# Half of the odd layer's weight sums made during the attention, six loads issued earlier, three adds moved to DVE

## The chip, the cores and the metric

The program runs on one core of a Trainium2 chip. The metric is the device time of one execution in microseconds. PE is the matrix engine; its weight loads (PEld) overlap with its matmuls. DVE, ACT and POOL are the vector, scalar and general engines. SP issues nearly all transfers. Each engine takes its instructions strictly in the order that was fixed when the program was built; semaphores alone hold it back.

## What is computed

Two layers on x of 1024 tokens by 1024 features, all in float32.

- Even layer: one input projection gives a_x, a_g, q, k, v, g. Path A puts a_x through a causal convolution of width 4 and a gated linear recurrence (RG-LRU, 8 blocks of 128 features). Path B is stick-breaking attention in 8 heads of 128. Each path is multiplied by its SiLU gate, and both together go through an output projection of 2048 by 1024.
- Odd layer: grouped-query attention in a window of 128 tokens (16 heads of 64, 2 key and value heads), gated, and an output projection of 1024 by 1024.
- After each layer x becomes LayerNorm(alpha * x + sublayer(x)), with a gain and a bias that are read from memory.

```
h = _rg_lru(_causal_dwconv(a_x, conv_w, conv_b), ...) * silu(a_g)
o = _stick_breaking(q, k, v) * silu(g)
x = _layer_norm(alpha * x + concat(h, o) @ w_out, g0, b0)
x = _layer_norm(alpha * x + _odd_layer(x) @ w_out_odd, g1, b1)
```

## The kernel before, in words

**Numbers.** Every product is made of three matmuls: each operand is split into a high part h (a cast on ACT) and a remainder l (a subtraction on DVE or POOL), and `mm3` adds h·h, h·l and l·h in one PSUM bank. A typical matmul is 128x128 by 128x512.

**Stages.** (1) Loading x and the first v products. (2) The recurrence: `lru_main(f)` for f = 0 to 7 makes gates and scan of block f, while PE is filled from a queue (`fill`) with the projections of block f+1 (`lru_proj`) and products for v (`v_tiles`). A projection fills a PSUM bank `pj_ax` or `pj_ag`; ACT reads it into `xc` (L489), DVE adds three shifted copies (L494), and the bank is free again. There are three such banks. (3) `attn_all`: 8 heads, whose 12 units each run scores `z`, sigmoid tiles B and C, a scan on C, B times C (L381, DVE), transposes `tr` (L389, PE), and products `pv` with v; the fill queue holds the projections k, q and g of the next head, and in head 7 the beginning of the output projection (`early_out`). (4) The output projections, in seven products of block sums (as in Strassen's scheme), into banks `opeX`, `opeZ` (even) and `opoX`, `opoZ`, `opoY` (odd), each followed by a LayerNorm. Between them lies the odd attention.

**Sums of weights.** The seven products need sums of blocks of the output weights. `odd_parts()` makes those of the odd layer in four groups t = 0 to 3: it loads four blocks into `oqta` and `oqtb`, makes sums and differences on POOL (L286 to L299), splits seven of them (`part`: cast on ACT L263, subtraction on POOL L264), and stores each in memory (`stoB..`, `stoT..`), from where the odd output projection reads them. The split parts lie in tiles with the tag `wt`, two at a time. The generator is advanced at each of the 32 steps of the recurrence, so all four groups stand in stage (2).

**First operands.** `prep(k)` loads the pair `opwh`, `opwl` of a step of the even output projection (512 KB each for k below 8, L575). `early_out()` is a generator in the fill queue of head 7; its first act is prep(0) to prep(7).

**Last norm.** `norm(s)` for the row tile s (128 tokens) takes the statistics (L711, L724 on DVE), the factors `rs` (L727, L728), scales on ACT (L732), multiplies by the gain on POOL (L733, 128x1024), and adds the bias one tile later in `shift()` (L718, 128x1024, on POOL in the last norm). The order is 4, 5, 6, 7, 0, 1, 2, 3; tile 3 alone is finished in pieces (L733 and L737 on POOL, L740 and L744 on DVE). The gain and bias lie in `gb2`.

The order of each engine's instructions is decided by a scheduler from the program and its own estimate of times, so a line that is moved in the code moves more than itself.

Of the kernel before, what the change touches and what calls it, by code (L numbers as in the profile page):

```python
# [13 lines left out]
F32R = mybir.dt.float32r  # L14
# [4 lines left out]
P = 128  # L19
S = 1024  # L20
D = 1024
# [31 lines left out]
def trunk(ctx, tc, x, xT_in, w_even, w_even_v, w_even_out, w_gate, lru_vec,  # L53
          e_ln, w_odd, sinks, w_odd_out, o_ln, out):
    nc = tc.nc
# [10 lines left out]
    def slot(name, dtype):  # L66
        return slots.tile([P, 2, HALF], dtype, tag="s", name=name)
# [200 lines left out]
    def odd_parts():  # L268

        sub = partial(nc.gpsimd.tensor_tensor, op=ALU.subtract)  # L270
        for t in range(4):
            p1, p2 = slot(f"oq{t}a", F32), slot(f"oq{t}b", F32)
            b11, b12, b21, b22 = p1[:, 0, :], p1[:, 1, :], p2[:, 0, :], p2[:, 1, :]
            for tile_, dm, e in ((b22, 1, 4 + t), (b12, 1, t), (b11, 0, t), (b21, 0, 4 + t)):
                nc.sync.dma_start(tile_, w_odd_out[dm, e])
            hold = []

            def part(kind, raw):
                if not hold:
                    two = yt("wt", [P, 2, 2, HALF], f"op{kind}{t}")  # L280
                    hold.extend([two[:, 0], two[:, 1]])
                stash_parts(kind, t, raw, hold.pop(), nc.gpsimd)

            part("oB22", b22)
            yield
            sub(out=b22, in0=b22, in1=b12)  # L286
            part("oT3", b22)
            yield
            part("oB11", b11)
            yield  # L290
            sub(out=b12, in0=b12, in1=b11)
            part("oT1", b12)
            yield
            nc.gpsimd.tensor_tensor(out=b11, in0=b22, in1=b11, op=ALU.add)
            part("oT2", b11)
            yield
            part("oB21", b21)
            yield
            sub(out=b21, in0=b21, in1=b11)  # L299
            part("oT4", b21)  # L300
            yield
            yield
# [43 lines left out]
    def attn_all():  # L346
# [8 lines left out]
        def u_stage(n, i, g):  # L355
            W = min(HALF, (i + 1) * P - g * HALF)
            z = bank("z", f"z{n}_{i}_{g}")
            qh, ql = qk["q", n, i // 4]
            kh, kl = qk["k", n, g]
            c = (i % 4) * P  # L360
            diag = (i // 4 == g)
            a, b = qh[:, c:c + P], ql[:, c:c + P]
            nc.tensor.matmul(z[:, :W], a, kh[:, :W], start=True, stop=False)
            nc.tensor.matmul(z[:, :W], a, kl[:, :W], start=False, stop=False)
            nc.tensor.matmul(z[:, :W], b, kh[:, :W], start=False, stop=True)
            if diag:
                nc.vector.tensor_tensor(out=z[:, W - P:W], in0=z[:, W - P:W], in1=mask, op=ALU.add)  # L367
            B = wt_("B", f"B{n}_{i}_{g}", F32)
            C = wt_("C", f"C{n}_{i}_{g}", F32, HALF + 1)
            nc.scalar.activation(C[:, :W], z[:, :W], AF.Sigmoid, scale=-SC)  # L370
            nc.scalar.activation(B[:, :W], z[:, :W], AF.Sigmoid, scale=SC)
            if diag:
                nc.gpsimd.memset(C[:, W:W + 1], 1.0)
                init = 1.0
            else:
                nc.vector.tensor_copy(C[:, W:W + 1], carry[n, i])
                init = carry[n, i]
            cr = C[:, 0:W][:, ::-1]
            nc.vector.tensor_tensor_scan(cr, cr, one.broadcast_to([P, W]), init, ALU.mult, ALU.mult)  # L379
            carry[n, i] = C[:, 0:1]  # L380
            nc.vector.tensor_tensor(out=B[:, :W], in0=B[:, :W], in1=C[:, 1:W + 1], op=ALU.mult)  # L381
            wsb[n, i, g] = B
# [41 lines left out]
        for idx in range(len(units) + LAG + 1):  # L424
            while vpend:
                v_stage(*vpend.pop(0))
            if idx < len(units):
                n, i, g = units[idx]
                if (i, g) == (NS - 2, 1) and n < 7:
                    w_sums(n + 1, w_even_out, 8)  # L430
                if n == 0 and (i, g) == (2, 0):
                    w_sums(0, w_even_out, 8)
                if (i, g) == (NS - 1, 1):
                    fill.drain()
                    load_ya(n)
                    fill.add(gate_proj(n, 1))
                    if n + 1 < SB_HEADS:
                        load_v(n + 1)
                        fill.add(gate_proj(n, 0), head_proj(n + 1))
                        rate[0] = 31.2 / 12  # L440
                        if n + 2 == SB_HEADS:
                            fill.add(gate_proj(n + 1, 0))
                            rate[0] = 36.4 / 12
                    else:
                        fill.add(early_out())
                        rate[0] = 20.8 / 12
                u_stage(n, i, g)
                pend.append(units[idx])
            if idx >= LAG and pend:
                n, i, g = pend.pop(0)  # L450
                t_stage(n, i, g)
                if i % 2 == 0 and g == 0:
                    vpend.append((n, i // 2))
            yield
# [182 lines left out]


    def early_out():
        for t in range(8):  # L640
            prep(t)
        for p in range(3):
            op[0, p] = bank(XB[p], f"opeX{p}")
        for t in range(8):
            for p in range(3):
                step_mm(t, p)
                yield C_512
# [18 lines left out]
    for f in range(8):  # L666
        q, sts = VT[f]
        if f == 2:
            for d in range(ND):
                load_wv(1, d)  # L670
        if f + 1 < 8:
            if f == 2:
                fill.add(lru_proj(f + 1), v_tiles(q, sts))
            else:
                fill.add(v_tiles(q, sts[:1]), lru_proj(f + 1), v_tiles(q, sts[1:]))
        else:
            fill.add(v_tiles(q, sts))
            load_v(0)
            fill.add(head_proj(0))
        r = (5.2 * len(sts) + 20.8) / 4  # L680
        for _ in lru_main(f):
            fill.pump(r)
            next(odd_w, None)
        fill.drain()
    for _ in attn_all():
        fill.pump(rate[0])
# [12 lines left out]
    def out_norms(lnp, gb, after, name, final):  # L699
# [13 lines left out]
        def shift():  # L713
            if pend:
                s = pend.pop()
                xt = xpre[:, s, :]
                eng = nc.gpsimd if final else nc.vector
                eng.tensor_tensor(out=xt, in0=xt, in1=gb[:, 1, :], op=ALU.add)  # L718
                after(s, slice(0, D))

# [352 lines left out]

    ep = ctx.enter_context(tc.tile_pool(name="epool", bufs=1, reuse_waits="tile"))
    gb2 = ep.tile([P, 2, D], F32, name="gb2")
    nc.sync.dma_start(gb2, o_ln.rearrange("(o a) d -> o a d", o=1).broadcast_to([P, 2, D]))
    put, norm, shift = out_norms(
        ep, gb2, lambda s, cs: nc.sync.dma_start(out[s * P:(s + 1) * P, cs], xpre[:, s, cs]), "o", True)

# [8 lines left out]
    y_diffs_odd()  # L1088
    for k in range(8, 12):
        prep_odd(k)  # L1090
    for p in range(4):
        evac_odd(0, p)
    for p in range(4):
# [72 lines left out]
```

## Time and profile before

| what | value |
|---|---|
| median of 3 runs | 1264.69 us (1263.58 to 1265.02) |
| profiled execution | 1261.55 us, of which the traced span is 1259.7 us |
| mean granted TensorE clock | 0.992 of full speed |
| PE busy | 1217.9 us, 97% of the span |
| DVE, POOL, ACT busy | 864.8 us (69%), 707.8 us (56%), 646.5 us (51%) |
| stage 2, the recurrence | about 60 to 333 us from the span's start |
| from the end of PE's last matmul to the end of the span | 1246.5 to 1259.7 us, 13.2 us |
| POOL in the last norm | at work without a break from 1220.1 to 1250.7 us |
| stage 3, one head of attention | 50.25 us (head 1: 401.86 to 452.11 us) |

The span is the time from the first to the last traced instruction; the 1.85 us beside it are start and end of the program. A share of 97% is a mean: where PE has no work that is ready, the stretch shows it, and that is what the rows further down are about.

### The profile page before, as it was taken

Reading aid. Unit: us, or ns where it says so; the run is one execution under the profiler, and the core shown is the slowest. Engines: PE = TensorE matmul, PEld = TensorE weight load, DVE = VectorE, ACT = ScalarE, POOL = GpSimd, SP = SyncE. Lnnn points to the kernel's source line nnn. Section 1 sums busy time; section 2 is a strip of 40 time slices with the busy share of each in tenths; the row PEclk is TensorE's granted clock in tenths of the full one; section 3 lists DMA queues with packets and bytes.
Section 4 is the critical chain, followed back from the end, with each engine's and each line's share of the span. In section 5 each row is a group of like instructions: output and inputs, shape, how many; then the busy total and the mean of one; then the engine's idle time right before and its main releaser. Section 6 shows DMA issues by size and latency. Waiting matters only on the chain.

```text
span 1259.7 us, 18357 instructions
## 1 busy us (share of the span) xinstructions
PE 1217.9 (97%) x6104; PEld 1027.3 (82%) x6104; DVE 864.8 (69%) x1589; ACT 646.5 (51%) x1309; POOL 707.8 (56%) x758
## 2 busy tenths in 40 slices
PE   8999989899999999999999999999999999999895
PEld 6788768688888888888888788888888888888684
DVE  7655656656677767677676848877447766666886
ACT  6355566666534434344343437443457776667432
POOL 3554578754474665564543258767256665544428
PEclk9999999999999999999999999999999999999998
DMA  8422655542654352552544789811010111104633
GB/s 293 196 77 89 237 213 209 197 138 89 204 167 134 134 178 74 176 179 76 183 138 153 280 319 334 263 49 50 26 51 27 34 35 34 43 1 135 233 120 132
DMA packets 95998, 179.50 MB, mean 142 GB/s; under 512 B 10912, under 2 KB 28704, under 8 KB 95648
## 3 DMA queue, kind: packets, MB, share of 16 engines
q1 hardware_dynamic: 95904, 178.34, 41.4%
q8 instruction: 48, 0.79, 0.3%
q14 instruction: 46, 0.38, 0.1%
HBM read 119.58 MB, written 58.72 MB: 142 GB/s over the span
## 4 chain that ended last, share of the span: by engine, by line
PE 85%; DVE 6%; DMA 3%; ACT 2%; issue 1%; POOL 1%; SPq 0%; POOLq 0%; ACTq 0%; DVEq 0%
PE tr L389 2%; PE pj_og L111 2%; PE pj_q L112 2%; PE pj_q L110 2%; PE pj_k L110 2%; PE pj_k L112 2%; PE pj_og L110 2%; PE pj_oq L110 2%; PE pj_og L112 2%; PE pj_oq L112 2%; PE pj_oq L111 2%; PE pj_k L111 2%; PE pj_q L111 2%; PE pj_g L112 2%; PE pj_g L111 2%; PE pj_g L110 2%
## 5 line engine op out<-in xcount | busy, mean ns | idle before, releaser
L370 ACT ACTIVATE C<-z 128x512 f32<-128x512 f32 (+3 forms) x96 | 47.4, 494 | 108.7 <-DVE z L367 68.7
L980 POOL TENSOR_SCALAR S<-S,sm 128x256 f32<-128x256 f32 (+1 forms) x128 | 57.7, 472 | 75.4 <-DVE sm L976 58.9
L582 POOL TENSOR_TENSOR opwl<-rawwl,opwl 128x512 fp32r<-128x512 f32 x48 | 75.3, 1592 | 27.5 <-ACT opwl L580 27.4
L973 ACT ACTIVATE S<-S,sm 128x256 f32<-128x256 f32 (+1 forms) x128 | 61.9, 485 | 37.3 <-DVE sm L966 37.1
L381 DVE TENSOR_TENSOR B<-B,C 128x512 f32<-128x512 f32 (+3 forms) x96 | 74.0, 772 | 10.2 <-DVE C L379 0.5
L582 DVE TENSOR_TENSOR opwh<-rawwh,opwh 128x512 fp32r<-128x512 f32 x48 | 66.3, 1418 | 20.9 <-ACT opwh L580 20.9
L379 DVE TENSOR_TENSOR_SCAN C<-C,one 128x512 f32<-128x512 f32 (+1 forms) x64 | 58.2, 909 | 21.7 <-ACT C L370 21.6
L379 DVE TENSOR_TENSOR_SCAN C<-C,C,one 128x512 f32<-128x512 f32 x32 | 45.7, 1427 | 32.3 <-ACT C L370 32.3
L118 ACT CAST wt<-tr 128x512 fp32r<-128x512 f32 (+3 forms) x96 | 46.4, 484 | 31.2 <-PE tr L389 30.8
L733 POOL TENSOR_TENSOR xpre<-xpre,gb 128x1024 f32<-128x1024 f32 (+1 forms) x16 | 39.2, 2456 | 39.7 <-ACT xpre L732 39.5
L418 POOL TENSOR_TENSOR yb<-pvt,yb 128x128 f32<-128x128 f32 x32 | 16.4, 513 | 78.9 <-DVE pvt L417 78.9
L110 PE MATMUL pj_ag<-xh,wh_ag 128*128 128x512 f32 x128 | 51.3, 401 | 9.3 <-DVE xc L494 7.0
L110 PE MATMUL pjv<-wv,xh 128*128 128x512 f32 x128 | 49.8, 400 | 10.0 <-ACT wv L219 5.3
L119 DVE TENSOR_TENSOR wt<-tr,wt 128x512 fp32r<-128x512 f32 (+3 forms) x96 | 52.4, 546 | 9.5 <-ACT wt L118 9.1
L957 DVE CUSTOM_DVE_ANT_0 S<-s,bias 128x256 f32<-128x256 f32 (+1 forms) x128 | 47.2, 403 | 16.1 <-PE s L950 10.2
L110 PE MATMUL pj_g<-xh,wh_g 128*128 128x512 f32 x128 | 52.8, 413 | 0.0
L110 PE MATMUL pj_q<-xh,wh_q 128*128 128x512 f32 x128 | 51.9, 406 | 0.0
L110 PE MATMUL pj_k<-xh,wh_k 128*128 128x512 f32 x128 | 51.9, 405 | 0.0
L112 PE MATMUL pj_g<-xh,wl_g 128*128 128x512 f32 x128 | 51.8, 404 | 0.0
L110 PE MATMUL pj_ax<-xh,wh_ax 128*128 128x512 f32 x128 | 50.1, 391 | 1.4 <-DVE gg L508 1.3
L110 PE MATMUL pj_oq<-x1h,wh_oq 128*128 128x512 f32 x128 | 51.0, 398 | 0.0
L111 PE MATMUL pjv<-wv,xh 128*128 128x512 f32 x128 | 50.8, 397 | 0.0
(383 smaller groups left out, 4449.2 us busy)
## 6 DMA issues: line engine op xcount, KB each, us to landing
vst<-vhl SPq DMA_DIRECT2D x16, 512.0 KB, 3.9
rawwh<-stS SPq DMA_DIRECT2D x32, 256.0 KB, 3.9
rawwl<-stT SPq DMA_DIRECT2D x32, 256.0 KB, 4.1
oopw<-stoT SPq DMA_DIRECT2D x16, 512.0 KB, 4.8
oopw<-stoB SPq DMA_DIRECT2D x12, 512.0 KB, 5.1
xraw<-in_xT_dram SPq DMA_DIRECT2D x16, 256.0 KB, 5.4
wvraw<-in_w_even_v_dram SPq DMA_DIRECT2D x16, 256.0 KB, 4.5
wr_ax<-in_w_even_dram SPq DMA_DIRECT2D x16, 256.0 KB, 3.2
```

The source lines that it names most:

```text
L110: nc.tensor.matmul(ps, wh, xh, start=start, stop=False)
L111: nc.tensor.matmul(ps, wh, xl, start=False, stop=False)
L112: nc.tensor.matmul(ps, wl, xh, start=False, stop=stop)
L118: nc.scalar.copy(h, ps)
L119: nc.vector.tensor_tensor(out=l, in0=ps, in1=h.bitcast(F32), op=ALU.subtract)
L370: nc.scalar.activation(C[:, :W], z[:, :W], AF.Sigmoid, scale=-SC)
L379: nc.vector.tensor_tensor_scan(cr, cr, one.broadcast_to([P, W]), init, ALU.mult, ALU.mult)
L381: nc.vector.tensor_tensor(out=B[:, :W], in0=B[:, :W], in1=C[:, 1:W + 1], op=ALU.mult)
L582: eng.tensor_tensor(out=hl[:, 1, :], in0=raw, in1=hl[:, 0, :].bitcast(F32), op=ALU.subtract)
L957: nc.vector.tensor_tensor_reduce(out=Sb[:, j, lo:], in0=ps[:, j, lo:], in1=bias[:, j, lo:], scale=1.0, scalar=-BIG, op0=ALU.add, op1=ALU.m ...
L973: nc.scalar.activation(Sv[:, j, los[v]:], Sv[:, j, los[v]:], AF.Exp, bias=nm[:, v, j:j + 1], accum_out=den[:, v, j:j + 1])
L980: nc.gpsimd.tensor_scalar(out=Sv[:, j, los[v]:], in0=Sv[:, j, los[v]:], scalar1=rec[:, v, j:j + 1], scalar2=0.0, op0=ALU.mult, op1=ALU.add)
```

## The change

There are four edits.

1. `odd_parts()` is advanced at every second step of the recurrence, so that groups 0 and 1 are made there. Groups 2 and 3 are advanced in heads 1 to 4, at units i = 6, 5, 4, 2. The split parts of groups 2 and 3 have tiles of their own from the large pool (`slot`) in place of the two `wt` tiles.
2. prep(0) to prep(2) are called at the start of head 7, ahead of the fill queue; `early_out()` calls prep(3) to prep(7).
3. In the last norm `shift()` of tiles 5, 7 and 1 runs on DVE in place of POOL.
4. The load of `gb2` is written behind `prep_odd(8)` to `prep_odd(11)` in place of ahead of the last products.

```diff
@@ odd_parts
             def part(kind, raw):
-                if not hold:
+                if t >= 2:
+                    hold.append(slot(f"op{kind}{t}", F32R))
+                elif not hold:
                     two = yt("wt", [P, 2, 2, HALF], f"op{kind}{t}")
@@ attn_all
                     else:
+                        for t in range(3):
+                            prep(t)
                         fill.add(early_out())
                         rate[0] = 20.8 / 12
                 u_stage(n, i, g)
+                if 0 < n < 6 and i in (6, 5, 4, 2) and g == 0:
+                    next(odd_w, None)
                 pend.append(units[idx])
@@ early_out
-        for t in range(8):
+        for t in range(3, 8):
             prep(t)
@@ the recurrence
-        for _ in lru_main(f):
+        for j, _ in enumerate(lru_main(f)):
             fill.pump(r)
-            next(odd_w, None)
+            if j % 2:
+                next(odd_w)
@@ shift
-                eng = nc.gpsimd if final else nc.vector
+                eng = nc.gpsimd if final and s not in (5, 7, 1) else nc.vector
@@ the last norm
-    nc.sync.dma_start(gb2, o_ln.rearrange("(o a) d -> o a d", o=1).broadcast_to([P, 2, D]))
...
     for k in range(8, 12):
         prep_odd(k)
+    nc.sync.dma_start(gb2, o_ln.rearrange("(o a) d -> o a d", o=1).broadcast_to([P, 2, D]))
```

**ACT in the recurrence.** These rows are ACT's order between the end of a v product (`vhl`, the cast of the finished bank) and the evacuation of the next projection (`xc_0`, `xc_1`, read from `pj_ax`), before the change. `opoT` and `opoB` are the split parts of the odd weights, `oq1` and `oq2` the blocks of groups 1 and 2.

```order
L118 CAST vhl_1428<-pjv_0_1398 128x512
L526 ACTIVATE ri_0_1_1448<-g_0_1_1444,vec 128x512
L263 CAST opoT_1654<-oq1b 128x512
L263 CAST opoB_1794<-oq2b 128x512
L118 CAST vhl_1475<-pjv_1_1450 128x512
L526 ACTIVATE ri_1_0_1514<-g_1_0_1510,vec 128x512
L526 ACTIVATE ri_1_1_1520<-g_1_1_1516,vec 128x512
L263 CAST opoB_1794<-oq2b 128x512
L489 ACTIVATE xc_0_1534<-pj_ax_0_1491,vec 128x512
L263 CAST opoB_1927<-oq2a 128x512 x2
L501 CAST xch_0_1541<-xc_0_1534 128x512
L489 ACTIVATE xc_1_1570<-pj_ax_1_1545,vec 128x512
```

The same place after the change; line numbers are shifted by about six.

```order
L532 ACTIVATE ri_0_0_1410<-g_0_0_1406,vec 128x512
L532 ACTIVATE ri_0_1_1416<-g_0_1_1412,vec 128x512
L263 CAST opoT_2612<-oq1b 128x512
L118 CAST vhl_1443<-pjv_1_1418 128x512
L532 ACTIVATE ri_1_0_1476<-g_1_0_1472,vec 128x512
L532 ACTIVATE ri_1_1_1482<-g_1_1_1478,vec 128x512
L495 ACTIVATE xc_0_1496<-pj_ax_0_1459,vec 128x512
L507 CAST xch_0_1503<-xc_0_1496 128x512
L495 ACTIVATE xc_1_1532<-pj_ax_1_1507,vec 128x512
L507 CAST xch_1_1542<-xc_1_1532 128x512
```

Every cast from `oq2` is gone between `vhl` and `xc`; the last cast of group 1 stays where it was. The rest of groups 2 and 3 (14 casts on ACT, 22 operations on POOL, 8 loads and 14 stores in all) leaves the recurrence in the same way. In DVE's order beside this, the remainder of the v bank (`vhl`, L119) now stands ahead of the difference `s3` of block 2 (L555), behind which it stood.

**ACT in head 1.** These rows are the same engine's order in head 1 after the change, where `wt` are transposed attention weights, `C` and `B` sigmoid tiles, `qh` a projection.

```order
L118 CAST kh_0_3659<-pj_k_0_3563 128x512
L372 ACTIVATE C_4_0_3690<-z_4_0_3685 128x512
L373 ACTIVATE B_4_0_3689<-z_4_0_3685 128x512
L118 CAST wt_5_0_3706<-tr_5_0_3701 128x4x128
L263 CAST opoT_3579<-oq2b 128x512
L263 CAST opoB_3696<-oq2a 128x512
L118 CAST qh_1_3724<-pj_q_1_3675 128x512
L118 CAST wt_5_1_3650<-tr_4_1_3740 128x128
L263 CAST opoT_3773<-oq2a 128x512
L372 ACTIVATE C_3_0_3734<-z_3_0_3728 128x512
```

The three casts from `oq2` are new there; the other rows stood in the same order before. On POOL the subtractions and the sums of `oq2` come between the resets and splits of this head. Heads 2, 3 and 4 take the remaining casts in the same way, group 3 in heads 3 and 4.

**SP at the start of head 7.** First before the change: the loads of `yain` for this head, loads for later steps (`rawwh`, `rawwl`), a store that waits for the head's result `yb`, and then the first pair of the output projection.

```order
L327 DMA yain_6795<-stA_2773 128x512
L327 DMA yain_6795<-stS_2777 128x512
L579 DMA rawwh_7344<-stS_1676 128x512
L579 DMA rawwl_7349<-stT_4065 128x512
L579 DMA rawwh_7354<-stS_1949 128x512
L579 DMA rawwl_7359<-stT_4628 128x512
L260 DMA stA_6861<-yb_6283 128x512
L575 DMA opwh_6895<-stA11p_770 128x1024
L575 DMA opwl_6897<-stB11p_3248 128x1024
```

After the change, on the same queue:

```order
L329 DMA yain_6801<-stA_2689 128x512
L329 DMA yain_6801<-stS_2693 128x512
L581 DMA opwh_6804<-stA11p_760 128x1024
L581 DMA opwl_6806<-stB11p_3164 128x1024
L581 DMA opwh_6808<-stA11p_1044 128x1024
L581 DMA opwl_6810<-stB11p_2837 128x1024
L581 DMA opwh_6812<-stA11p_1346 128x1024
L581 DMA opwl_6814<-stB11p_3423 128x1024
L585 DMA rawwh_7350<-stS_1634 128x512
L585 DMA rawwl_7355<-stT_4009 128x512
L585 DMA rawwh_7360<-stS_1897 128x512
L260 DMA stA_6879<-yb_6289 128x512
```

Six loads of 512 KB stand ahead of that store and of the four `raw` loads. On PE the first matmuls of `opeX` stand right behind the last matmul of the gate (`pj_g`) in head 7, ahead of the scores of unit (6, 0); before the change they stood behind the scores of unit (2, 0), six units later. The load of `gb2` stands at the same place of SP's order in both kernels.

**The last norm.** On DVE the add L725 (before: L718 on POOL) stands between the add of bank `opoX3` and the statistics of tile 7 for tile 5, behind the first statistics of tile 1 for tile 7, and ahead of the first statistics of tile 3 for tile 1. POOL has the other five adds and all multiplications, in the order in which it had them.

## Rows read from the trace of the kernel before

**Rows 1.** The page's list of engines: busy time, share of the span, instructions.

```profile
PE 1217.9 (97%) x6104; PEld 1027.3 (82%) x6104; DVE 864.8 (69%) x1589; ACT 646.5 (51%) x1309; POOL 707.8 (56%) x758
```

**Rows 2.** Busy time by engine in stretches of the recurrence and of head 7.

```profile
core 0: us, PE busy (x) PEld busy (x) DVE busy (x) ACT busy (x) POOL busy (x), PEclk, DMA share, GB/s
157.00:189.00 32.00, 25.81 (x113) 20.66 (x111) 18.48 (x18) 20.37 (x28) 24.93 (x21) 0.98 0.56 210
187.90:194.73 6.83, 5.78 (x14) 4.55 (x15) 5.98 (x10) 2.53 (x5) 6.83 (x7) 0.50 0.88 340
220.00:252.00 32.00, 27.51 (x119) 21.79 (x118) 21.44 (x26) 19.79 (x28) 25.40 (x23) 1.00 0.54 199
697.00:724.00 27.00, 24.15 (x146) 20.42 (x145) 23.50 (x51) 13.97 (x35) 7.17 (x12) 1.00 0.81 302
```

**Rows 3.** PE's timeline: start, duration, line, and in brackets idle time ahead, releaser.

```profile
152.15 0.47 PE L110 MATMUL pjv<-wv,xh 128*128 128x512 f32 x1 [1.65 <-DVE xc L494]
...
179.40 0.47 PE L110 MATMUL pj_ag<-xh,wh_ag 128*128 128x512 f32 x1 [2.36 <-DVE vhl L119]
...
188.95 0.77 PE L110 MATMUL pj_ag<-xh,wh_ag 128*128 128x512 f32 x1 [3.83 <-DVE xc L494]
...
237.38 0.48 PE L110 MATMUL pjv<-wv,xh 128*128 128x512 f32 x1 [3.11 <-DVE xc L494]
...
244.40 0.47 PE L110 MATMUL pj_ax<-xh,wh_ax 128*128 128x512 f32 x1 [1.27 <-DVE gg L508]
```

**Rows 4.** ACT's groups at 178 to 241 us: busy, mean ns, idle ahead, releasers.

```profile
L263 ACT CAST opoB<-oq2b 128x512 fp32r<-128x512 f32 x2 | 1.2, 618 | 7.2 <-POOL oq2b L286 4.1 <-issue 3.1
...
L263 ACT CAST opoT<-oq3a 128x512 fp32r<-128x512 f32 x1 | 0.6, 621 | 3.7 <-DMA stoT<-opoB 3.7
L263 ACT CAST opoT<-oq2b 128x512 fp32r<-128x512 f32 x2 | 1.2, 611 | 3.6 <-DMA stoT<-opoB 3.6
...
L263 ACT CAST opoB<-oq3a 128x512 fp32r<-128x512 f32 x2 | 1.2, 622 | 2.0 <-POOL oq3a L291 2.0
```

**Rows 5.** DVE's timeline ahead of PE's idle time at 177 us.

```profile
176.91 1.75 DVE L555 TENSOR_TENSOR s<-gg,gg 128x512 f32<-128x512 f32 x1
```

**Rows 6.** Head 1: its stretch (columns as in rows 2), then timelines of POOL, DVE, PE.

```profile
401.86:452.11 50.25, 50.25 (x276) 43.10 (x274) 35.97 (x63) 20.38 (x47) 27.36 (x32) 1.00 0.42 142
...
424.85 0.62 POOL L102 TENSOR_SCALAR wh_k<-wr_k 128x512 fp32r<-128x512 f32 x1 [3.96 <-PE pj_q L111]
...
428.26 0.56 DVE L381 TENSOR_TENSOR B<-B,C 128x384 f32<-128x384 f32 x1
...
433.52 0.49 PE L389 MATMUL tr<-ident,B 128*128 128x128 f32 x3
```

**Rows 7.** SP's timeline in head 7, PE's there, and the median time to land.

```profile
689.44 0.46 SPq L327 DMA_DIRECT2D yain<-stS  x1
...
703.83 0.43 SPq L575 DMA_DIRECT2D opwh<-stA11p  x1
...
698.25 0.40 PE L363 MATMUL z<-kh,qh 128*128 128x512 f32 x1
...
opwh<-stA11p SPq DMA_DIRECT2D x8, 512.0 KB, 9.1
```

**Rows 8.** DVE's timeline in the last norm, and the adds L718 (min/median/max ns).

```profile
1222.68 2.19 DVE L728 SCALAR_TENSOR_TENSOR rs<-mv,rs 128x1 f32<-128x1 f32 x1
...
1248.25 2.83 DVE L740 SCALAR_TENSOR_TENSOR xpre<-xpre,mv,gb 128x384 f32<-128x384 f32 x1
...
1251.80 0.61 DVE L740 SCALAR_TENSOR_TENSOR xpre<-xpre,mv,gb 128x384 f32<-128x384 f32 x1
...
L718 DVE TENSOR_TENSOR xpre<-xpre,gb x8: 1210/1541/3426, 837.3 to 883.2; 128x1024 f32<-128x1024 f32 x8
L718 POOL TENSOR_TENSOR xpre<-xpre,gb x7: 2354/2400/2648, 1224.8 to 1253.0; 128x1024 f32<-128x1024 f32 x7
```

**Rows 9.** The chain of waits at its end: start, duration, engine, tile, line.

```profile
1252.99 2.61 POOL xpre L718
```

## The prediction

> **What bounds the kernel now.** I read the page's list of engines first, then the busy time by stretch, then PE's timeline for what ends each of its idle times, and last the engines named there. PE is busy for 1217.9 us of a span of 1259.7 us [rows 1], so an edit can only pay where PE has no work, or behind its last matmul at 1246.5 us. The attention heads have no such place: in head 1 PE is busy for all of 50.25 us [rows 6]. The recurrence has: PE loses 32.00 - 25.81 = 6.19 us at 157 to 189 us and 4.49 us at 220 to 252 us, and head 7 loses 2.85 us of 27 [rows 2]. PE's timeline names the reasons: waits of 2.36, 3.83, 3.11 and 1.27 us that DVE's `vhl`, `xc` and `gg` end [rows 3]. None of these is DVE's own slowness. DVE works on `xc` as soon as ACT has written it at L489, and ACT stands still in this stretch in front of casts of odd weights: 7.2, 3.6, 3.7 and 2.0 us, together 16.5 us, for POOL's sums or for stores that free the `wt` tiles [rows 4]. Since ACT works in order, the evacuation of a finished projection bank waits behind such a cast, and PE finds no free bank. A second cost follows: right after the waits of 2.36 and 3.83 us the granted clock of TensorE falls to 0.50 (its 1.2 GHz level) for 6.83 us [rows 2], which costs 6.83 / 2 = 3.4 us.
>
> **The recurrence.** The order of ACT shows that all casts of groups 2 and 3 leave the places ahead of `xc`. What each wait is worth:
> - 2.36 us: DVE's order puts `vhl` ahead of `s3`, which took 1.75 us [rows 5]. That much goes: 1.75.
> - 3.83 and 3.11 us: both end with `xc` at L494, behind ACT's blocked casts. Both go whole: 6.94. That they go whole is a choice; the wait of 1.65 us at 152 us is ended by the same line, and the casts near it (group 1) stay, so it stays.
> - Half clock: 3.4, as the idle time ahead of it shrinks from 6.19 to 0.61 us.
> - 1.27 us behind `gg`: one link further from the casts; I take half, 0.6.
>
> The sum is 1.75 + 6.94 + 3.4 + 0.6 = 12.7 us. Bounds: at most 2.36 + 3.83 + 3.11 + 1.27 + 3.4 = 14.0. At least half of the two large waits plus the clock, 3.5 + 3.4 = 6.9, if DVE, ACT and the recurrence's own chain are late by themselves once the casts are gone. ACT is busy for 20.4 of 32 us there and DVE for 18.5 [rows 2], both far from full, which is why I take a value near the upper end.
>
> **Heads 1 to 4.** Here 14 casts and 22 operations of POOL come in, with 8 loads and 14 stores of SP's queue. An ACT cast takes 0.62 us [rows 4], 3.5 casts a head 2.2 us, and ACT is busy for 20.4 of 50.25 us. POOL gets 5.5 operations a head. The split that POOL does for the next head waits 3.96 us for PE [rows 6], so POOL is ahead there. I have no row of the new operations in a head; the nearest is the 27.36 us for 32 operations of POOL in head 1 [rows 6], 0.86 us each, which makes 4.7 us a head, spread over four places. What would be late next is B times C on DVE and then the transpose on PE: B is ready at 428.82 and read at 433.52 us, 4.7 us of slack [rows 6]. A head's whole work at one place would just use up this slack, and in four places it does not reach PE. I take 0. If the cover is gone at one place of each head and 1.5 us come through, that is +6.0 us, the upper bound; a gain has no room, since PE is never idle there.
>
> **Stores and loads.** The parts of groups 2 and 3 are read in the odd output projection, hundreds of us later, so their landing costs nothing. The head moves 142 GB/s at a DMA share of 0.42 [rows 6], against 340 GB/s and 0.88 in the recurrence [rows 2], so transfers are not the limit. The parts have tiles of their own, so no cast waits for a store. 0.
>
> **Head 7.** The first pair is issued at 703.83 us, behind a store that waits for the head's result; after the change it stands right behind the load issued at 689.44 us [rows 7]. So PE has matmuls of `opeX` to put between the units at once. The landing took 9.1 us in the median, when sixteen loads came together; 689.9 + 9.1 = 699.0 us, and PE asks for them where the scores of unit (6, 0) start, 698.25 us [rows 7]. So a first wait of up to 0.8 us is possible, but only two of the six loads are needed first. 2.85 us of idle time lie in the stretch that is filled, and I take all of it; the bounds are 0 (four `raw` loads and the store of the head's result, now behind six loads, give the time back) and 2.85.
>
> **The last norm.** Three adds of 2.40 us leave POOL; on DVE the same shape took 1.21 us at the least, 1.54 in the median and 3.43 at the most [rows 8]. DVE and POOL hinder each other: a DVE operation on 128x1 took 2.19 us and one on 128x384 2.83 us, where the same line alone took 0.61 us [rows 8], each time until POOL's running operation had ended. The Trainium skill, GPSIMD Engine Reference, section 1 (Specifications), says that POOL shares its SBUF interfaces with DVE and that they contend where a DVE instruction has two SBUF inputs. By that rule the trace agrees (2.83 against 0.61 us), and an add moved to DVE still keeps POOL out while it runs. So the moved adds stand in front of the statistics that DVE owes to the chain, and the time that POOL saves (3 x 2.40) comes back in part as DVE's own work and waits. Working the order through with these durations, I get from 1.4 us earlier to 1.1 us later at the end, by who gets in first. I take 0. The outer bound is a gain of 4.7: the 2.83 us become 0.61 (2.2), and the add of 2.61 us near the chain's end [rows 9] is done before the last tile's own pieces, with L733 directly followed by L737 (2.5 of it, as 0.1 us of start remains). The load of `gb2` keeps its place in the queue: 0.
>
> **Sum.** 12.7 + 2.85 = 15.5 us. The profiled execution took 1261.55 us, so 1246.0 us in its terms; the median of the runs is 3.1 us higher, 1264.69, and the prediction is 1264.69 - 15.5 = 1249.2 us.
>
> **Rivals.**
> - *The last norm comes free as well.* For it speaks that POOL is the engine that works without a break from 1220 us and loses 7.2 us of work; against it the three DVE adds in front of the chain. 1249.2 - 4.7 = 1244.5 us. The Trainium skill, GPSIMD Engine Reference, section 8 (Key points), puts DVE at about twice POOL's speed for elementwise work; by that rule the move is a gain, and the trace agrees at the least duration (1.21 against 2.40 us) but not at the median.
> - *Another chain takes over in the recurrence*, and only 6.9 us come: 1264.69 - 6.9 - 2.85 = 1254.9 us. For it speaks the wait of 1.65 us at L494 with few casts near [rows 3]; against it the low busy shares.
> - *The heads pay.* 1.5 us a head: 1249.2 + 6.0 = 1255.2 us.
> - *Nothing moves*, because the casts weren't what ACT's neighbours waited for: 1264.7 us. Against it, 16.5 us of ACT's waits in one stretch.
> - *Slower: the waits move along with the casts.* ACT stands 16.5 us in front of the same casts, now in heads 1 to 4, where `wt`, B and C come late behind it and PE has no slack; with one new spell of half clock, 3.4 us, that is 19.9 - 15.5 = +4.4, 1269.1 us. It decides from 15.5 + 2.5 = 18.0 us, 4.5 us a head. Against it: 7.3 of these 16.5 us were waits for stores that freed `wt`, and the new tiles wait for no store.
>
> **How the numbers follow.** A difference under 0.2%, 2.5 us, is about what a measurement of this kernel can't tell from none. Chances: the forecast 0.60, the free last norm 0.12, the other chain 0.12, paying heads 0.08, nothing 0.03, slower 0.05. Faster is the first four, 0.92; same 0.03; slower 0.05. The range goes from the full gain with a free last norm (14.0 + 2.85 + 4.7 = 21.5 below, 1243.2, rounded to 1243.5) to the least gain of the recurrence with nothing from head 7 (1264.69 - 6.9 = 1257.8, taken as 1257.5), and leaves out nothing moving and slower, with a little at either end.
>
> **What would show it.** In the changed kernel's profile: PE busy for at least 30 of 32 us at 157 to 189 and at 215 to 247 us, no stretch at clock 0.5 near 188 us; no wait of ACT at L263 in the recurrence; heads 1 to 4 at 50.2 to 50.4 us each; no idle time of PE in head 7 over 0.8 us ahead of the first `opeX`; from PE's last matmul to the end of the span 13.2 us as before, give or take 1.4. The prediction is wrong if heads 1 to 4 grow by over 1 us each, if PE's waits for L494 remain without the casts, or if the last norm shrinks by over 3 us.

## The result, and the profile after

| | before | changed |
|---|---|---|
| median | 1264.13 us (1262.71 to 1265.02, 4 runs) | 1249.51 us (1247.97 to 1250.44, 4 runs) |
| profiled execution | 1261.55 us, span 1259.7 us | 1249.07 us, span 1247.3 us |

The ratio is 0.9884, with a 95% interval of 0.9867 to 0.9901: 14.6 us faster, at 1249.5 us where 1249.2 us had been forecast. The sum came out; its terms did not. To see that, I cut each span at the same matmuls: the first one, the first scores of each head, the first matmul of `opeZ`, the end of the last one. All of these are starts and ends on PE's timeline; a stretch is the difference of two of them.

| stretch (us) | before | changed | difference | forecast |
|---|---|---|---|---|
| first matmul to head 0 (recurrence) | 328.39 | 313.75 | -14.64 | -12.7 |
| heads 1 to 4 | 200.98 | 204.77 | +3.79 | 0 |
| head 7's first scores to the first `opeZ` | 51.03 | 51.89 | +0.86 | -2.85 |
| end of the last matmul to the end of the span | 13.18 | 11.43 | -1.75 | 0 |
| all else (0.55 of it ahead of the first matmul) | 666.12 | 665.45 | -0.67 | 0 |
| span | 1259.70 | 1247.29 | -12.41 | -15.5 |

The profiled execution of before was one of its quicker ones, 2.6 us under its median, and that of the changed kernel 0.4 us under its own; so the two profiles show 12.4 us of the 14.6.

The busy times of the changed kernel in five stretches: two of the recurrence, head 1, the end of head 7, and what follows the last matmul.

```profile
core 0: us, PE busy (x) PEld busy (x) DVE busy (x) ACT busy (x) POOL busy (x), PEclk, DMA share, GB/s
157.00:189.00 32.00, 31.87 (x141) 25.96 (x140) 23.20 (x27) 20.18 (x28) 23.05 (x19) 1.00 0.48 181
215.00:247.00 32.00, 32.00 (x142) 26.39 (x141) 19.96 (x29) 19.56 (x25) 15.39 (x16) 1.00 0.29 91
368.65:421.85 53.20, 51.17 (x273) 43.02 (x272) 37.11 (x59) 21.69 (x51) 38.27 (x39) 1.00 0.54 188
720.86:726.30 5.44, 4.41 (x15) 3.44 (x14) 1.87 (x4) 5.13 (x11) 4.19 (x4) 0.69 0.32 108
1235.86:1247.29 11.43, 0.00 (x1) 0.00 (x0) 7.57 (x11) 1.15 (x3) 7.15 (x4) 0.61 0.36 138
```

The first two answer to [rows 2]: PE's idle time of 6.19 and 4.49 us is gone but for 0.13 us, and so is the half clock near 190 us. The third is head 1 from its own first scores to those of head 2. The stretch of [rows 6] is a head's length too, but begins 18 us inside head 1; from first scores to first scores (383.85 to 434.08 us) head 1 of the kernel before took 50.23 us, with 27.33 us of POOL. POOL's work in it rose to 38.27 us, and PE lost 2 us outright. The fourth stretch is new: a mean granted clock of 0.69, at the end of head 7. PE's timeline shows the idle times ahead of both new losses, and the one of [rows 3] that stayed:

```profile
151.35 0.47 PE L110 MATMUL pjv<-wv,xh 128*128 128x512 f32 x1 [1.61 <-DVE xc L500]
...
415.32 0.63 PE L391 MATMUL tr<-ident,B 128*128 128x128 f32 x4 [0.88 <-DVE B L383]
...
419.87 0.39 PE L409 MATMUL pv<-wt,vh 128*128 128x256 f32 x1 [1.11 <-DVE wt L119]
...
720.29 0.36 PE L408 MATMUL pv<-wt,vh 128*128 128x256 f32 x1 [0.90 <-DVE pvt L419]
...
722.10 0.47 PE L599 MATMUL opeX<-opwl,opwh 128*128 128x512 f32 x1 [1.03 <-DVE pvt L419]
```

In head 1 PE waits for B, which the prediction had seen 4.7 us early, one unit later [rows 6]. ACT's timeline shows why it is late:

```profile
405.73 0.62 ACT L263 CAST opoT<-oq2b 128x512 fp32r<-128x512 f32 x1 [1.71 <-POOL oq2b L288]
...
409.99 0.62 ACT L263 CAST opoT<-oq2a 128x512 fp32r<-128x512 f32 x1 [2.46 <-POOL oq2a L293]
410.51 0.59 ACT L372 ACTIVATE C<-z 128x512 f32<-128x512 f32 x1
```

It is the picture of [rows 4], moved into the head: ACT stands in front of two moved casts until POOL has made their sums, and the sigmoid tile C stands behind the second one.

### The profile page after: what moved, and what is told of

It is laid out like the page before. It is cut to its first block, busy times and chain, and to the rows that moved or that the text cites. A ratio compares the mean times of both kernels' runs of the same rounds, so it can differ in the third digit from the quotient of the medians.

```text
span 1247.3 us, 18357 instructions
## 1 busy us (share of the span) xinstructions
PE 1216.8 (98%) x6104; PEld 1026.2 (82%) x6104; DVE 871.9 (70%) x1592; ACT 644.0 (52%) x1308; POOL 710.1 (57%) x755
## 4 chain that ended last, share of the span: by engine, by line
PE 87%; DVE 4%; DMA 3%; POOL 2%; issue 1%; ACT 1%; SPq 1%; POOLq 0%; ACTq 0%; DVEq 0%
PE opeX L599 2%; PE opeX L600 2%; PE opeX L601 2%; PE pj_og L111 2%; PE pj_og L110 2%; PE pj_oq L110 2%; PE pj_og L112 2%; PE pj_oq L112 2%; PE pj_oq L111 2%; PE pj_g L112 2%; PE tr L391 2%; PE pj_g L110 2%; PE pj_g L111 2%; PE pj_q L112 2%; PE pj_k L110 2%; PE pj_k L112 2%
## 5 line engine op out<-in xcount | busy, mean ns | idle before, releaser
L383 DVE TENSOR_TENSOR B<-B,C 128x512 f32<-128x512 f32 (+3 forms) x96 | 79.0, 823 | 10.6
L381 DVE TENSOR_TENSOR_SCAN C<-C,one 128x512 f32<-128x512 f32 (+1 forms) x64 | 63.9, 999 | 29.1 <-ACT C L372 29.0
L964 DVE CUSTOM_DVE_ANT_0 S<-s,bias 128x256 f32<-128x256 f32 (+1 forms) x128 | 47.2, 403 | 15.9 <-PE s L957 10.2
L119 DVE TENSOR_TENSOR wt<-tr,wt 128x512 fp32r<-128x512 f32 (+3 forms) x96 | 52.3, 546 | 4.2 <-ACT wt L118 4.0
L110 PE MATMUL pj_q<-xh,wh_q 128*128 128x512 f32 x128 | 51.9, 406 | 0.0
L599 PE MATMUL opeX<-opwl,opwh 128*128 128x512 f32 x128 | 50.0, 398 | 1.0 <-DVE pvt L419 1.0
L111 PE MATMUL pjv<-wv,xh 128*128 128x512 f32 x128 | 50.8, 397 | 0.0
```

Of the source, the lines that this page charges most:

```text
L110: nc.tensor.matmul(ps, wh, xh, start=start, stop=False)
L111: nc.tensor.matmul(ps, wh, xl, start=False, stop=False)
L119: nc.vector.tensor_tensor(out=l, in0=ps, in1=h.bitcast(F32), op=ALU.subtract)
L599: f(b, y[:, 0, c], w[:, 0, :], start=fresh, stop=False)
L964: nc.vector.tensor_tensor_reduce(out=Sb[:, j, lo:], in0=ps[:, j, lo:], in1=bias[:, j, lo:], scale=1.0, scalar=-BIG, op0=ALU.add, op1=ALU.m ...
```

## The experiments

Times in brackets are ranges of the runs; the ratio is to the kernel before, run on the same chip. Its median there was 1262.67 us for the next four kernels, 1264.15 us for `spread3`, `prep1`, `spread_prep1` and `slots_lru`, and 1262.64 us for the last four. Stretches are cut as above, each from one profile.

**Each edit alone.** The kernel before with edit 1, with edit 2, and with edit 3, as they stand in the diff above.

> Edit 1 alone on the kernel before. Theory: edit 1 alone gives the whole gain of the recurrence (328.4 us from PE's first matmul to head 0 become 313.8, -14.6) and is alone at fault for head 1 (50.2 becomes 53.2, +3.0) and for 0.2 to 0.4 us in each of heads 2 to 4; head 7 (51.0) and the stretch behind PE's last matmul (13.2) stay. Time -10.8 us, 1253.3 us. Rival A: part of the recurrence's gain came from elsewhere, so that it is 12.7 or less here. Rival B: head 1's loss was an accident of one execution, so head 1 takes 50.3 us and the time is 1250.4 us.

> Edit 2 alone on the kernel before. Theory: the matmuls of opeX are used up early, the end of head 7 has nothing to fill it, and the half-clock stretch there follows; from head 7's first scores to the first opeZ 51.9 us in place of 51.0, time +0.9, 1265.0 us. Rival (as predicted): the early pair fills the idle time, 48.2 us, time -2.85, 1261.3 us, and the loss at head 7's end in the changed kernel came from the other edits.

> Edit 3 alone on the kernel before. Theory: from the end of PE's last matmul to the end of the span 11.4 us in place of 13.2, time -1.7, 1262.4 us; nothing else moves. Rival: as predicted, nothing at the end (13.2 us, 1264.1 us), and the 1.7 us of the changed kernel came from another arrival of the last tiles.

| | median | ratio (95%) | the stretch that it is about |
|---|---|---|---|
| before | 1262.67 us | | |
| sums_only | 1251.82 us (1247.97 to 1252.85) | 0.9910 [0.9891, 0.9930] | recurrence 315.0, head 1 53.63, heads 2 to 4 151.15 |
| prep_only | 1264.49 us (1262.45 to 1267.37) | 1.0012 [0.9999, 1.0024] | head 7 to `opeZ` 52.97 |
| shift_only | 1260.41 us (1259.12 to 1262.87) | 0.9983 [0.9974, 0.9993] | after the last matmul 11.45 |

The three differences, -10.9, +1.8 and -2.3, make -11.3 of the 14.6; with intervals of 1.2 to 2.5 us each either way, the 3.3 us between them are within the noise. By stretches each edit does the same alone as together with the others: edit 1 gives the recurrence's gain (13.4 us here) and head 1's loss, edit 3 gives the end, and edit 2 gives no gain (its interval reaches from no change to 3 us slower). The profile of `prep_only` is also 3.3 us longer in the recurrence, which edit 2 doesn't touch; 13.6 us at half clock stand there, 6.8 us in the profile of before. As the scheduler brings the load of `gb2` to the same place in both kernels, edit 4 was not run by itself.

**Casts off ACT, in the heads.** The changed kernel, with the casts of groups 2 and 3 made by POOL.

```diff
-        nc.scalar.copy(hl[:, 0, :], raw)
+        if cast is not None:
+            cast(out=hl[:, 0, :], in0=raw, scalar1=1.0, scalar2=0.0, op0=ALU.mult, op1=ALU.add)
+        else:
+            nc.scalar.copy(hl[:, 0, :], raw)
...
-                stash_parts(kind, t, raw, hold.pop(), nc.gpsimd)
+                stash_parts(kind, t, raw, hold.pop(), nc.gpsimd,
+                            nc.gpsimd.tensor_scalar if t >= 2 else None)
```

> The changed kernel with the 14 casts of groups 2 and 3 made on POOL in place of ACT; PE's and DVE's orders stay as they were. Theory A: head 1 is longer because ACT stands 1.7 and 2.5 us in front of two casts that wait for POOL's sums, with the sigmoid tiles C and B behind them; without the casts on ACT, head 1 takes 50.3 to 50.6 us and the time is 2.5 to 3 us lower, about 1246.8 us. Rival B: head 1 is longer because POOL has 38 in place of 27 us of work and holds up DVE's scans; POOL now gets 14 more operations, so head 1 takes 53.2 us or more, and heads 2 to 4 over 50.6, time 1249.5 us or above.

Measured: 1250.34 us (1247.72 to 1252.91), 0.9904 [0.9884, 0.9924]. Head 1 took 50.53 us, as theory A has it: the sigmoid tile C of unit (3, 0) starts 39.2 us into the head in place of 41.9. Heads 2 and 4 took 52.43 and 52.39 us, as rival B has it. The timelines of DVE and PE show B's side in head 2, which begins at 418.3 us; PE waits for DVE where DVE waits for POOL's queue, which is late with its resets of C and its remainders:

```profile
421.82 1.37 DVE L387 TENSOR_TENSOR B<-B,C 128x128 f32<-128x128 f32 x1 [1.15 <-POOL C L379]
...
423.74 0.36 PE L412 MATMUL pv<-wt,vh 128*128 128x256 f32 x1 [0.74 <-DVE pvt L423]
...
428.38 0.63 PE L395 MATMUL tr<-ident,B 128*128 128x128 f32 x4 [0.65 <-DVE C L382]
```

So each was half right: the blocked casts make head 1 long, and more work on POOL makes other heads long.

**Three steps a head in place of four.** The changed kernel with one step less in each head, over five heads.

```diff
-                if 0 < n < 6 and i in (6, 5, 4, 2) and g == 0:
+                if 0 < n < 6 and i in (6, 4, 2) and g == 0:
```

> The changed kernel with three steps of groups 2 and 3 in each of heads 1 to 5 (units i = 6, 4, 2) in place of four in heads 1 to 4. PE's and DVE's orders stay; on ACT the cast opoT1 no longer stands ahead of C and B of unit (3, 0) in head 1. Theory A (ACT's wait of 2.5 us for that cast is what reaches PE): head 1 takes 50.4 to 50.7 us, heads 1 to 5 together 252.3 to 253.0 us in place of 255.2, time 2.5 us lower than the changed kernel's, about 1247.0 us. Rival B (what counts is POOL's work as a whole): the loss moves to another head, as it did with the casts on POOL, heads 1 to 5 together 254.5 us or more, time 1249 us or more.

Measured: 1245.34 us (1244.24 to 1246.65), 0.9855 [0.9838, 0.9872]. Heads 1 to 5 together took 251.22 us, exactly as before the change, where the changed kernel took 255.02 (the expectation's 255.2 was 0.2 too high). The order of ACT differs in head 1 by one row, the cast `opoT1` that stood ahead of C. In this kernel's head 1 DVE has its scan and B, and then PE its transposes, at

```profile
410.71 1.62 DVE L381 TENSOR_TENSOR_SCAN C<-C,one 128x512 f32<-128x512 f32 x1 [0.48 <-ACT C L372]
412.46 1.50 DVE L383 TENSOR_TENSOR B<-B,C 128x512 f32<-128x512 f32 x1
...
415.25 0.60 PE L391 MATMUL tr<-ident,B 128*128 128x128 f32 x4
```

B is ready at 413.96 us and read at 415.25: 1.3 us of slack are left. That is theory A's side, and no other head became longer, as rival B would have it; the move of the sums into the heads is free at three steps a head (in all four profiles with them) and not at four. What this run doesn't part is ACT's cast from POOL's work: the remainder that belongs to the cast leaves this place on POOL as well.

**One early pair in place of three.** The changed kernel with prep(0) alone ahead of the fill queue.

```diff
-                        for t in range(3):
+                        for t in range(1):
                             prep(t)
...
-        for t in range(3, 8):
+        for t in range(1, 8):
```

> The changed kernel with prep(0) alone ahead of the fill queue (prep(1) to prep(7) stay in early_out). On PE two groups of opeX stand early, one more a little later, and the rest between the units of head 7's second half and its end. Theory A (there is a fixed amount of fill, which the changed kernel spends too early, so that the end runs dry and half clock follows): from head 7's first scores to the first opeZ 49.5 us in place of 51.9, time 2.4 us lower than the changed kernel's, about 1247.1 us. Rival B (the idle time only moves to the middle, where it was before): 50.8 to 51.2 us, time 1248.6 us. Rival C: early loads don't matter at all, the loss stays at 51.9 us.

Measured: 1247.44 us (1244.20 to 1250.74), 0.9871 [0.9843, 0.9900]. From head 7 to the first `opeZ` it took 49.2 us, of which PE was busy for 47.74, at full clock:

```profile
676.03:725.25 49.22, 47.74 (x268) 40.83 (x267) 32.97 (x71) 23.73 (x58) 14.49 (x20) 1.00 0.71 258
```

Theory A holds (49.5 expected), and the three other profiles with one pair have the same 49.2 us. Of the 2.7 us against the changed kernel about 1.0 is PE's idle time (1.5 us here, 2.5 us with three pairs); most of the rest comes with the half clock, without which three pairs took 50.3 us in three other profiles. With three pairs all 72 matmuls of `opeX0` to `opeX2` stand ahead of the transposes of unit (2, 0); with one pair 36 of them stand behind these, between the last products `pv`.

**Both.** The last two edits together.

> The changed kernel with both: three steps in each of heads 1 to 5, and prep(0) alone ahead of the fill queue. The two places lie apart (heads 1 to 5, head 7), so the differences add: by theory A of both -2.5 - 2.4 = 4.9 us below the changed kernel's time, about 1244.6 us; by rival B of both about 1248.5 us or more.

Measured: 1243.96 us (1242.86 to 1246.17), 0.9846 [0.9827, 0.9865]; heads 1 to 5 251.22 us, head 7 49.21 us. By stretches the differences add.

**Tiles of their own, in the recurrence.** The kernel before, with only the first hunk of edit 1 (`if t >= 2: hold.append(slot(...))`).

> The kernel before with the tiles of edit 1 alone: groups 2 and 3 stay in the recurrence, but their parts lie in tiles of their own, so no cast waits for a store. Theory A (ACT's waits for stores, 7.3 of 16.5 us, and for POOL's sums, 6.1 us, each delay xc): about half of the gain of the recurrence, 328.4 us from PE's first matmul to head 0 become 321 to 323, time 6 us lower than before, about 1257 us. Rival B: the two tiles alone were the cause; 313.5 to 316 us, 13 to 14 us lower. Rival C: POOL's sums alone were the cause; 327 to 329 us, no difference.

Measured: 1271.47 us (1270.96 to 1272.79), 1.0060 [1.0040, 1.0079], and 338.8 us for the recurrence. None of the three had a loss. ACT's groups at 178 to 275 us show the reason:

```profile
L263 ACT CAST opoB<-oq3b 128x512 fp32r<-128x512 f32 x2 | 1.2, 622 | 7.5 <-DMA stoT<-opoT 7.5
L263 ACT CAST opoT<-oq2b 128x512 fp32r<-128x512 f32 x2 | 1.2, 622 | 11.7 <-DMA stoB<-opoB 9.4 <-POOL oq2b L301 2.3
...
L263 ACT CAST opoT<-oq3a 128x512 fp32r<-128x512 f32 x2 | 1.2, 614 | 8.7 <-DMA stoT<-opoT 8.7
```

The casts wait for stores as before, and longer, 30.5 us in this stretch in place of 7.3: the pool of 27 tiles hands a part the place of an earlier part, whose store has not ended. Tiles by name are not free tiles.

**Casts off ACT, in the recurrence.** The kernel before with the same casts on POOL as in the heads above.

> The kernel before with the 14 casts of groups 2 and 3 made on POOL in place of ACT; they stay in the recurrence, with the two wt tiles, and POOL gets 14 operations more. PE's order stays. Theory A (as predicted: ACT's standing in front of these casts is the whole cause): from PE's first matmul to head 0 313 to 316 us in place of 328.4, time 13 us lower than before, about 1251 us. Theory B (POOL's sums and the waits for stores hold up the recurrence in another way too, as POOL also makes the recurrence's own products and the splits of weights): 320 us or more, time above 1256 us.

Measured: 1262.46 us (1257.10 to 1266.21) beside 1262.64 us of before, 1.0001 [0.9987, 1.0015]; the recurrence took 332.5 us. By the time rival B is right; the waits show more. ACT has no moved cast any more, and PE's two waits of 3.83 and 3.11 us behind `xc` [rows 3] are gone; after 1.69 us at 154 us PE has no wait for `xc` left in the recurrence. That is theory A's mechanism. `slots_lru` shows it from the other side: where ACT stood longer in front of its casts, PE's waits for `xc` from 140 us on rose from 8.6 to 13.6 us. But POOL, with 14 operations more, brought other waits, and PE's idle time in the recurrence is 15.9 us in place of 15.4 (the rest of the 4.1 us is half clock, 13.7 us of it in place of 6.8):

```profile
213.86 0.50 PE L110 MATMUL pj_ax<-xh,wh_ax 128*128 128x512 f32 x1 [1.97 <-DVE gg L512]
...
234.94 0.50 PE L112 MATMUL g<-xch,wl_gate 128*128 128x512 f32 x1 [1.30 <-POOL wl_gate L103]
```

The longest one, followed back over POOL's square `xc`, DVE's `t`, to PE:

```profile
242.04 1.04 POOL L541 TENSOR_TENSOR xc<-ri 128x512 f32<-128x512 f32 x1
...
243.12 1.74 DVE L542 SCALAR_TENSOR_TENSOR t<-xc,t 128x512 f32<-128x512 f32 x1 [5.19 <-POOL xc L541]
...
245.61 0.74 PE L110 MATMUL pj_ax<-xh,wh_ax 128*128 128x512 f32 x1 [4.03 <-DVE gg L512]
```

POOL makes the recurrence's own products (here L540, L541), and works at that place through sums, casts and remainders of group 3 first; ACT had written the input of L541 by 232.5 us, and POOL came to it at 242.0. DVE waits 5.2 us for `xc`, `gg` stands next behind it, and a PSUM bank stays full. The wait of 1.97 us has another reason. DVE's `t`, which takes 0.68 us elsewhere in this profile, began as soon as its `xc` was there and ended when POOL paused, after ten operations without a break (203.00 to 212.67 us); `gg` came at 213.13 us:

```profile
203.09 10.12 DVE L542 SCALAR_TENSOR_TENSOR t<-xc,t 128x512 f32<-128x512 f32 x1 [5.91 <-POOL xc L541]
```

In the kernel before DVE has no wait of 0.4 us or more for POOL between 140 and 300 us, though beside POOL it took 3.56 us for two such `t` ahead of the `gg` that PE waits 1.27 us for. So this run shows that POOL has no room for the casts; that POOL's sums alone held up the kernel before is not shown. What taking the casts off ACT would give without more work for POOL was not tried.

**Once more, side by side.** The changed kernel, the version with both edits, and the latter with `eng = nc.vector` for all seven adds of the last norm.

> The changed kernel once more, beside the next one on the same chip. Theory: head 1 takes 53.1 to 53.7 us again, so its loss belongs to the order and not to one execution; head 7 to the first opeZ takes 50.3 us where the waits of 0.9 and 1.0 us at its end are not followed by half clock, 51.9 us or more where they are. Time 1249.5 us. Rival: head 1 at 50.3 us, an accident.

> The version with three steps in each of heads 1 to 5 and prep(0) alone ahead of the fill queue, beside the changed kernel on the same chip. Theory: heads 1 to 5 together 251.2 us, head 7 49.2 us, time 5.5 us below the changed kernel's, about 1244.0 us. Rival: the earlier difference was one between the calls, and the two agree within 2.5 us.

> The last version with all seven adds of the last norm on DVE in place of three. Theory A (DVE and POOL take turns, and an add costs 1.2 us on DVE and 2.4 us on POOL, so every add moved shortens the turn): from PE's last matmul to the end of the span 10 to 11 us in place of 11.4, time 1243 us. Rival B (DVE's adds now stand in front of the statistics and pieces of the last tile): 12 to 14 us, time 1245 us or more.

| | median | ratio (95%) |
|---|---|---|
| before | 1262.64 us | |
| changed_again | 1251.23 us (1248.17 to 1255.03) | 0.9914 [0.9897, 0.9932] |
| best_again | 1243.47 us (1243.28 to 1245.41) | 0.9854 [0.9838, 0.9871] |
| shift_all | 1247.92 us (1246.16 to 1248.41) | 0.9883 [0.9869, 0.9897] |

The version with both edits is 7.8 us faster than the changed kernel, more than the 5.5 expected; the intervals of the two lie apart. In the profile of `changed_again` head 1 took 50.77 us, against the 53.1 expected for the same order. The next fences show the same two rows of DVE and POOL in head 1, first of the changed kernel, then of `changed_again`.

```profile
411.14 2.41 DVE L381 TENSOR_TENSOR_SCAN C<-C,one 128x512 f32<-128x512 f32 x1 [2.66 <-ACT C L372]
...
411.14 1.32 POOL L264 TENSOR_TENSOR opoB<-oq2a,opoB 128x512 fp32r<-128x512 f32 x1
```

```profile
414.81 1.23 DVE L381 TENSOR_TENSOR_SCAN C<-C,one 128x512 f32<-128x512 f32 x1 [2.65 <-ACT C L372]
...
414.86 2.27 POOL L264 TENSOR_TENSOR opoB<-oq2a,opoB 128x512 fp32r<-128x512 f32 x1
```

The one that gets in first takes 1.2 to 1.3 us, and the other ends about 1.1 us after it. Where POOL got in first, the scan was 1.2 us late and the head took 2.4 us more. Head 3 of the changed kernel shows the same in one execution: there the scan began 0.03 us ahead of POOL, and the head took 50.5 us without idle time of PE, though ACT had stood 2.40 us in front of the same cast:

```profile
514.68 1.22 DVE L381 TENSOR_TENSOR_SCAN C<-C,one 128x512 f32<-128x512 f32 x1 [2.64 <-ACT C L372]
```

ACT's waits in front of the casts were much the same in both kernels; they use up the slack, and what is lost goes with the order of arrival. So the theory was right about the cause and wrong in calling the size fixed: 53.2, 53.6 and 53.2 us in three kernels with that order of instructions (the scan took 2.40 or 2.41 us in each), 50.8 us in the fourth.

`shift_all` settles the last norm for rival B: 13.4 us behind the last matmul in place of 11.4. (Another 1.8 us of its profile, 96.9 in place of 95.1 us from the first `opoX` to the last matmul, come with half clock near 1160 us, ahead of the first add: 10.24 us of it here, 3.41 us in the profile of `best_again`.) Its chain of waits:

```profile
1233.93 2.59 POOL xpre L740
...
1236.54 1.23 DVE xpre L725
1237.77 0.13 DVE mv L731
```

The add of tile 2 waits on DVE for POOL's multiplication, and the last step of tile 3's statistics (`mv`), the last ones, stands behind it. The Trainium skill, GPSIMD Engine Reference, section 8 (Key points), puts DVE at about twice POOL's speed in elementwise work; the trace agrees for most of the adds here (six of seven took 1.20 to 1.23 us on DVE, where `best_again` has 2.40 to 3.26 us on POOL), less for the three adds on DVE in the changed kernel (1.21, 2.31 and 3.40 us beside a busy POOL). The kernel with all seven adds on DVE is slower all the same.

## Why the prediction was right, and where it was wrong

**The recurrence** (12.7 forecast, 14.6 measured; 12.2 to 15.5 in eight other profiles with edit 1, against the 328.4 us of before; two further profiles with the old order, `shift_only` and `prep_only`, had 328.6 and 331.7 us). All four waits went whole, the one behind `gg` too, and the one behind `vhl` with its last 0.6 us: PE's idle time fell by 10.6 us. The half clock was priced too high, as PE was busy for only 5.78 of those 6.83 us [rows 2]; that makes 2.9 us and not 3.4. The other 1.1 us stand at no wait over 0.15 us. The mechanism as written, that "DVE works on `xc` as soon as ACT has written it" and that ACT's blocked casts are what delays PE, is borne out: PE's waits for `xc` rose where ACT stood longer (`slots_lru`) and went where the casts left ACT (`pool_cast_lru`). How the gain divides between the 14 casts and POOL's 22 operations stays open, since no run took the casts off ACT without giving them to POOL. For 3.1 of the 16.5 us of ACT's waits the rows name neither a sum nor a store [rows 4].

**Heads 1 to 4** (0 forecast, +3.8 measured: 3.0 in head 1, 0.8 in the other three). The step that failed is "A head's whole work at one place would just use up this slack, and in four places it does not reach PE". The slack of 4.7 us was counted against POOL's time alone, and at unit (2, 0). The transposes that waited in the changed kernel are those of unit (3, 0), with 3.5 us of slack before, as DVE's and PE's timelines of the kernel before have it:

```profile
425.00 1.00 DVE L381 TENSOR_TENSOR B<-B,C 128x512 f32<-128x512 f32 x1
...
429.48 0.60 PE L389 MATMUL tr<-ident,B 128*128 128x128 f32 x4
```

ACT's casts were priced at their duration of 0.62 us, not at the 1.7 and 2.5 us for which ACT stands in front of them; and three of a head's steps came together on POOL between 403.5 and 414.6 us. The bound of +6 held. This is the mechanism of the slower rival, and its waits did move along with the casts: ACT stood in front of them for 6.1, 4.0, 5.9 and 3.8 us in heads 1 to 4. The longest in heads 2, 3 and 4 are

```profile
461.25 0.62 ACT L263 CAST opoT<-oq2b 128x512 fp32r<-128x512 f32 x1 [4.02 <-POOL C L375]
...
513.53 0.62 ACT L263 CAST opoT<-oq3a 128x512 fp32r<-128x512 f32 x1 [2.40 <-POOL oq3a L293]
...
562.24 0.62 ACT L263 CAST opoT<-oq3b 128x512 fp32r<-128x512 f32 x1 [3.78 <-POOL C L375]
```

The sum is 19.8 us (4.0 of it for loads of blocks), more than the 18.0 us at which that rival was to decide. What it had wrong is "PE has no slack": 2.0 us of idle time came through to PE, all of it in head 1.

**Head 7** (-2.85 forecast, +0.9 measured). The step that failed is "2.85 us of idle time lie in the stretch that is filled, and I take all of it". The matmuls of `opeX` are a fixed stock. The waits of the middle went, as forecast; those of 0.90 and 1.03 us came at the end, where the stock was gone, so PE's idle time from head 7's first scores to the first `opeZ` fell only from 2.7 to 2.5 us, and there half clock followed. With one early pair the stretch takes 49.2 us, so 1.8 us were to be had.

**The last norm** (0 forecast, with 1.4 earlier to 1.1 later; 1.75 earlier measured). The row of 2.83 us became 0.62, and POOL's add of 2.61 us left the chain, as the outer bound had it; of these 4.8 us DVE gave back 1.2 in front of the last statistics and 1.8 at another row that waits for POOL, as the chain of the changed kernel shows:

```profile
1235.44 1.13 DVE xpre L725
...
1239.63 1.98 DVE rs L735
...
1241.63 0.61 ACT xpre L739
...
1242.31 0.93 POOL xpre L740
```

**The sum.** The profiles differ by 12.4 us where 15.5 were forecast: 3.8 and 3.7 us too good in the heads and head 7, 1.9 and 1.75 too bad in the recurrence and at the end, and 0.67 elsewhere. That the medians hit the forecast to 0.3 us is those errors and the quick profiled execution of before taken together: luck, and not the steps. Four of the prediction's own signs were missed: heads 1 to 4 at 50.5 to 53.2 us where 50.2 to 50.4 had been named, a wait of ACT at L263 in the recurrence (2.67 us, for a sum of group 1), waits of 0.90 and 1.03 us in head 7 where at most 0.8 us was allowed, and an end 1.75 us shorter where 1.4 us was allowed.

## What to carry to other kernels

Work that is moved onto an engine which runs in order holds up what stands behind it for as long as the engine waits in front of it, not for as long as it takes; look at what makes its operand, and at how much slack stands behind it (here 19.8 us of such waits came with heads 3.8 us longer). A run that hands work from one engine to another changes both: read which waits went and which came before reading its time. Filling matmuls are a stock: to use them early is to miss them late, so count what is left for the last stretch, where a wait can cost clock as well.

## What the runs showed of the hardware

- A DVE scan and a POOL operation on SBUF meet in heads 1 and 3 of the four kernels with four steps a head. In five of these eight heads the scan began 0.03 or 0.04 us ahead, took 1.22 or 1.23 us, and the head 50.3 to 50.8 us; in three the two starts lay within 0.02 us, the scan took 2.40 or 2.41 us, and the head 53.2 to 53.6 us. The Trainium skill, Trainium Architecture — The Big Picture, section "What this means for kernel authors", calls the port pair of the two engines an exclusive lock and not a split of bandwidth; the trace agrees, since the one that got in first took 1.22 to 1.32 us in each of these heads.
- The one that comes late need not get in after one operation: a DVE operation that takes 0.68 us elsewhere took 10.12 us in `pool_cast_lru`, while POOL ran ten operations at their usual 0.64 to 1.32 us each. Why DVE did not get in between them is not shown. So it is not semaphores alone that hold an engine back.
- The same idle times of 0.90 and 1.02 to 1.03 us stand at the end of head 7 in five profiles with this order. In two of them a spell of half clock began there, in the changed kernel behind the second wait and in `prep_only` behind the first (51.9 and 53.0 us); in three none did (50.3 us each).
